# Rebuilding the FFN of a one-layer decoder step: fixed product banks, weight sums on VectorE, activations stored split

## The chip, the cores and the metric

The kernel runs on one core of a Trainium2 chip. The time is the device time of one execution in microseconds. The kernel before was timed in three runs: 3052.62, 3056.04 and 3064.1 us, the median 3056.04.

## The reference

One layer of a hybrid decoder is applied to 512 prompt tokens and to 32 sample tokens (8 sequences of 4) with the same weights; the model width is 2048 and everything is 32-bit floating point. Stick-breaking attention and a gated delta rule share one projection, cross-attention to a memory follows, then the feed-forward network (FFN), which alone changes here:

```python
hf = rmsnorm(x, p['norm_ffn_g'])
gate, up = jnp.split(hf @ p['w_gate_up'], 2, axis=-1)      # 2048 x 11264
x = x + (jax.nn.silu(gate) * up) @ p['w_down']             # 5632 x 2048
```

The kernel treats all 544 tokens (T) together, as two halves of 272 (HT), with features on the 128 partitions (P). There are 16 feature blocks of the model (KD) and 44 of the hidden layer (NH).

## The kernel before

Up to about 1505 us the kernel does the projections, the mixers and cross-attention; the change leaves these alone. The rest is the FFN.

**One wino.** The FFN multiplies 2x2 blocks by Winograd's form of Strassen's method: `wino` computes two blocks of columns of a weight matrix times all tokens, with seven products P1 to P7 instead of eight. Its inner dimension is given as a list of *pairs* of feature blocks. For each pair there are seven right operands (b11, b21, b22, and the sums t1 to t4), each of 128 x 272. For the weights `left` makes seven left operands: three are blocks of the matrix itself, four are sums s1 to s4. To get 32-bit accuracy from TensorE's fast format, each operand is kept as two exact parts, high and low, and each product is three matmuls: wh·bh, wh·bl, wl·bh.

**One unit.** `left` serves two pairs at a time: two DMAs of 256 KB on SP's queue into a tile `u`, four sums on POOL (L1613 to L1616), then two casts on ACT that give the high parts `wh` (L1620: 128x768 for the three blocks, 128x1024 for the four sums) and two subtractions on VectorE (DVE) that give the low parts `wl` (L1621, same shapes). The tiles of `wh` and `wl` have two buffers each. A unit is then 7 products x 2 pairs x 3 parts = 42 matmuls of 128x272 (L1647). There are 264 units.

**Gate-up.** 44 winos (j = 0 to 43), each over 8 pairs: 4 units, 168 matmuls. After each, `combine` (L1661 on ACT copies P1 out of PSUM; L1673 to L1679 on DVE add the other products) gives the gate and the up half, L1712 to L1715 apply scales and Silu. After each odd j two hidden blocks make a pair: POOL computes the sums t1 to t4 (`sums`, L1572 to L1575), and five transfers on ACT's queue store the pair in `hT` in DRAM, unsplit (L1719, L1721).

**Down.** The hidden pairs come in chunks of 4, 4, 4, 4 and 6 pairs (FFN_CHUNKS). For every chunk, 8 winos (m = 0, 2, ... 14) of two units (three in the last chunk) cover the 16 output blocks. `fetch` loads a pair from `hT` on SP's queue (L1696) and splits it again (L1590 on ACT, L1591 on DVE); two pairs of the next chunk are fetched at m = 4 and 10, the others at the chunk's end. From chunk 1 on `combine` adds the combined result to accumulators (DVE L1663 to L1669, POOL L1670 and L1671). In the last chunk the residual x is added on POOL, and `store_y` transposes, scales back and stores the blocks of the wino before.

**PSUM.** Eight banks: two buffers of a two-bank tile `mm`, and four one-bank buffers `aux`. The products lie in them as the code says:

```python
ma, mb = c.mm(), c.mm()
p4, p7, p3 = (c.aux()[:, :HT] for _ in range(3))
p1, p2, p6, p5 = ma[:, 0, :HT], ma[:, 1, :HT], mb[:, 0, :HT], mb[:, 1, :HT]
# (product, left operand, right operand)
todo = ((p1, 1, 0), (p2, 2, 1), (p4, 0, 6), (p6, 4, 4), (p5, 3, 3), (p7, 5, 5), (p3, 6, 2))
```

Each engine works through its own queue in order. A tile framework lays down that order and places the waits: an instruction waits for the last users of the tile's buffer that it writes, and for the writers of what it reads. `step` calls and priorities place the fetches and the next weights between the others.

Of the kernel before, what the change touches and what calls it, by code (L numbers as in the profile page):

```python
# [8 lines left out]
F32 = mybir.dt.float32  # L9
# [6 lines left out]
P = 128  # L16
# [17 lines left out]
PAIR_TAGS = [["ah"] * 7, ["ah"] * 5 + ["al"] * 2, ["al"] * 7, ["al"] * 3 + ["r"] * 4, ["ah"] * 4 + ["al"] * 3, ["al"] + ["h"] * 3 + ["t"] * 3, ["t"] * 7, ["t"] * 7]  # L34
# [36 lines left out]
def build_consts(c):  # L71
# [45 lines left out]
    # rows (head of two, 7 - batch, part, step) to columns (head of two, batch, step), both parts summed  # L117
# [4 lines left out]
    # rows (batch of four, part, head, step) to columns (head, batch of four, step): the head's own, both parts summed  # L122
# [17 lines left out]
def head_rows(c):  # L140
    """Per-head scalars: columns (chunk, head) on every partition, and two columns with rows (head, batch, step)."""
# [45 lines left out]
def weights(c, w, k0, nk, c0, n=P, kept=False, eng=None):  # L187
    """A block of weights, split exactly into two parts of 12 bits each: a pair for every feature block."""
# [13 lines left out]
def products(c, ps, w, k, act, first, last, n=P):  # L202
    """One block of a projection: w^T act, exact but for the product of the two low parts."""
# [11 lines left out]
def project(c, w, k0, c0, acts, n=P, step=8):  # L215
    """PSUM [n, 2, 272] = (rows k0.. of w, columns c0..c0+n)^T acts"""
# [14 lines left out]
def split(c, x, g, hi=None, lo=None):  # L231
    """x * g (g per partition) as two exact parts."""
# [13 lines left out]
class Stats:  # L246
    """Sum of squares over all features, for every token, on every partition."""
# [15 lines left out]
    def rstd(self, name, scale=None):  # L263
        """(mean + EPS) ** -0.5; with scale, what was added is scaled by it, and so is the root's reciprocal."""
# [81 lines left out]
def x_rstd(c, ss):  # L346
    """The reciprocal roots of the tokens' mean squares, from columns to rows on every partition."""
# [21 lines left out]
def first_projections(c):  # L369
    """Loads the tokens and projects them on the first head's q and k, feature block by feature block."""  # L370
# [20 lines left out]
class Side:  # L391
    """Work of the mixers, handed out in small steps between the blocks of the projections.

    A step yields (tensor engine time, time until its results are there), both estimates in us."""
# [6 lines left out]
    def put(self, g, low=False, tiles=None):  # L401
        """tiles: where the work takes its temporary tiles (float32, float32r) from, if not from the usual ones"""
# [51 lines left out]
    def finish(self, e, steps=1e9):  # L454
        """Runs one work to its end, or until so many of its steps are done."""
# [5 lines left out]
    def drain(self, some=None):  # L461
        """Runs all that is left, or until some is done."""
# [70 lines left out]
    # the sums of the keys behind, a block of keys after the other, each token's in its own column  # L533
# [21 lines left out]
def stick(c, z, n, sp=None):  # L555
    """softplus(z) and log(sigmoid(z)), each over n columns"""
# [18 lines left out]
def sb_sample(c, g):  # L575
    """Stick-breaking attention of the sample group, four heads: 512 paged keys and its own."""
# [12 lines left out]
    # own keys: rows (head, batch, step)  # L589
# [28 lines left out]
    # paged keys: columns (page, head, batch, step)  # L618
# [33 lines left out]
def parts(c, src, vector=True):  # L652
    """src [P, 512] as two exact parts."""
# [108 lines left out]
def load_pages(c, cache, pages, h0, nh):  # L762
    """[keys, (page, head, d)] of the given pages (indices into the table)."""
# [11 lines left out]
def gates(c, acts, rstd):  # L775
    """Decay and beta of the gated delta rule, with tokens on partitions."""
# [4 lines left out]
    # prompt: columns (a|b, chunk, head); sample: columns (a|b, stack), rows (head, batch, step)  # L781
# [28 lines left out]
    # running sums of log decay, totals, and their exponentials  # L810
# [22 lines left out]
    # per (head, batch) of the sample stacks, on every partition  # L833
# [7 lines left out]
def silu(c, x, out):  # L841
    """out = x * sigmoid(x), with exp and ln alone"""
# [1104 lines left out]
```

## Time and profile before

| | us |
|---|---|
| median of three runs | 3056.04 |
| span of the profiled execution (its own time beside which the parts are set) | 3059.9 |
| busy: PE / PE weight loads / DVE / ACT / POOL | 2900.2 / 2789.1 / 2134.3 / 1363.5 / 1671.8 |
| first to last start of the FFN's matmuls (L1647) | 1511.5 to 3047.9 |
| first to last copy of P1 in the gate-up (L1661, 44 of them) | 1545.4 to 2487.0 |

PE is TensorE, PEld its weight loads, which overlap the matmuls. A row of a group of instructions gives the line, the engine, the operation, the tiles (out<-in) and the shape, then the busy time and the mean duration in ns, then the idle time of the engine ahead of them and what ended it. A row of the timeline begins with the start in us from the span's start and the duration in us; what stands in brackets is the engine's idle time before, with the instruction that ended it. A row of a window gives its length, the busy time of PE, PEld, DVE, ACT and POOL with the number of instructions, the clock that TensorE was granted, the share of time in which the DMA engines were busy, and GB/s.

### The profile page before, as it was taken

What the parts mean: (1) busy time and instruction counts of PE and PEld (TensorE: products, weight loads), DVE (VectorE), ACT (ScalarE), POOL (GpSimd) and SP (SyncE); (2) the same over time, 40 slices, a digit from 0 to 9 for tenths busy, and PEclk for the clock granted to TensorE, in tenths of its full rate; (3) what the DMA queues carried; (4) which work ended last, traced back from release to release, by engine and by line L of the source; (5) the groups of instructions that cost most, each with busy time, mean ns of one, the idle gap of its engine ahead of it and who ended that gap; (6) DMA issues with size and microseconds to landing.
All of it is one profiled execution on the core that took longest, in us unless ns stands there. A gap on an engine that the chain in (4) does not pass through costs nothing.

```text
span 3059.9 us, 58347 instructions
## 1 busy us (share of the span) xinstructions
PE 2900.2 (95%) x22118; PEld 2789.1 (91%) x22118; DVE 2134.3 (70%) x3339; ACT 1363.5 (45%) x2600; POOL 1671.8 (55%) x1784
## 2 busy tenths in 40 slices
PE   8999999999999999999799999999999989988898
PEld 7999998889899999999689999999999989988797
DVE  6776775655655655366687777777777888888865
ACT  5544453435645654245543343333333344334333
POOL 3211122312112100032378988898888977999997
PEclk9999999999999999999899999999999999999999
DMA  7323233544535765423434344333434354344343
GB/s 212 95 80 85 75 88 99 144 137 147 173 105 151 227 197 150 127 81 116 161 117 127 118 122 123 121 117 118 125 118 123 116 179 132 110 131 127 119 137 105
DMA packets 619505, 392.67 MB, mean 128 GB/s; under 512 B 36475, under 2 KB 572360, under 8 KB 619224
## 3 DMA queue, kind: packets, MB, share of 16 engines
q1 hardware_dynamic: 596904, 355.95, 39.6%
q10 hardware_dynamic: 22320, 32.99, 3.0%
q8 instruction: 174, 2.85, 0.4%
q14 instruction: 107, 0.88, 0.1%
HBM read 334.17 MB, written 54.68 MB: 127 GB/s over the span
## 4 chain that ended last, share of the span: by engine, by line
POOL 27%; PE 20%; DVE 8%; issue 4%; DMA 4%; ACT 2%; SPq 0%; POOLq 0%; ACTq 0%; DVEq 0%
PE mm L208 7%; POOL u L1615 6%; POOL u L1613 6%; POOL u L1614 5%; PE mm L1647 5%; POOL u L1616 5%; PE aux L1647 4%; DVE wl L1621 3%; DMA u<-in_w_gate_up 2%; DVE pr L1591 2%; PE aux L1342 2%; POOL acc L1670 1%; PE mm L1530 1%; POOL x L1572 1%; PE aux L960 1%
## 5 line engine op out<-in xcount | busy, mean ns | idle before, releaser
L1621 DVE TENSOR_TENSOR wl<-u,wh 128x768 fp32r<-128x768 f32 (+1 forms) x528 | 752.5, 1442 | 315.9 <-ACT wh L1620 213.6
L1647 PE MATMUL mm<-pr,wh 128*128 128x272 f32 x4224 | 830.6, 292 | 41.6 <-DVE acc L1663 25.3
L1620 ACT CAST wh<-u 128x768 fp32r<-128x768 f32 (+1 forms) x528 | 488.8, 943 | 826.5 <-PE aux L1647 295.4
L1647 PEld LDWEIGHTS mm<-pr,wh 128*128 128x128 f32 x4224 | 669.4, 191 | 50.5 <-DVE acc L1663 20.3
L1647 PE MATMUL aux<-pr,wh 128*128 128x272 f32 x3168 | 626.9, 292 | 17.7 <-DVE acc L1669 6.7
L1647 PE MATMUL mm<-pr,wl 128*128 128x272 f32 x2112 | 615.7, 292 | 22.5 <-DVE wl L1621 22.5
L208 PE MATMUL mm<-ah,wh 128*128 128x272 f32 (+1 forms) x2464 | 538.6, 298 | 5.7 <-ACT ah L321 4.6
L1647 PEld LDWEIGHTS aux<-pr,wh 128*128 128x128 f32 x3168 | 506.8, 192 | 21.7 <-DVE acc L1669 8.6
L208 PE MATMUL mm<-al,wh 128*128 128x272 f32 (+1 forms) x2464 | 524.3, 291 | 0.7 <-DVE al L239 0.7
L208 PE MATMUL mm<-ah,wl 128*128 128x272 f32 (+1 forms) x2464 | 515.6, 290 | 0.1
L1647 PE MATMUL aux<-pr,wl 128*128 128x272 f32 x1584 | 460.9, 291 | 2.0 <-DVE wl L1621 2.0
L1647 PEld LDWEIGHTS mm<-pr,wl 128*128 128x128 f32 x2112 | 403.3, 191 | 28.4 <-DVE wl L1621 28.4
L208 PEld LDWEIGHTS mm<-ah,wh 128*128 128x128 f32 (+1 forms) x2464 | 391.9, 189 | 28.8 <-issue 8.5
L197 DVE TENSOR_TENSOR wl<-wr,wh 128x512 fp32r<-128x512 f32 (+1 forms) x366 | 264.0, 725 | 195.9 <-ACT wh L196 186.7
L208 PEld LDWEIGHTS mm<-al,wh 128*128 128x128 f32 (+1 forms) x2464 | 389.6, 188 | 5.4 <-issue 2.0
L208 PEld LDWEIGHTS mm<-ah,wl 128*128 128x128 f32 (+1 forms) x2464 | 386.2, 188 | 2.5 <-DVE wl L197 0.5
L196 ACT CAST wh<-wr 128x512 fp32r<-128x512 f32 (+1 forms) x366 | 224.3, 615 | 336.6 <-PE mm L208 272.6
L1613 POOL TENSOR_TENSOR u<-u 128x256 f32<-128x256 f32 x264 | 277.3, 1050 | 140.8 <-DMA u<-in_w_gate_up 90.2
L1615 POOL TENSOR_TENSOR u<-u 128x256 f32<-128x256 f32 x264 | 323.2, 1224 | 0.0
L1616 POOL TENSOR_TENSOR u<-u 128x256 f32<-128x256 f32 x264 | 308.5, 1169 | 19.1
L1647 PEld LDWEIGHTS aux<-pr,wl 128*128 128x128 f32 x1584 | 303.7, 192 | 2.6 <-DVE wl L1621 2.4
L1614 POOL TENSOR_TENSOR u<-u 128x256 f32<-128x256 f32 x264 | 270.4, 1024 | 0.0
(518 smaller groups left out, 3809.1 us busy)
## 6 DMA issues: line engine op xcount, KB each, us to landing
u<-in_w_gate_up SPq DMA_DIRECT2D x352, 256.0 KB
wr<-in_w_in SPq DMA_DIRECT2D x108, 512.0 KB
u<-in_w_down SPq DMA_DIRECT2D x176, 256.0 KB
v<-hT SPq DMA_DIRECT2D x66, 272.0 KB
page<-in_cache_sb_k SPq DMA_DIRECT2D x128, 128.0 KB
page<-in_cache_sb_v SPq DMA_DIRECT2D x64, 256.0 KB
wr<-in_w_out SPq DMA_DIRECT2D x32, 512.0 KB
hT<-x ACTq DMA_DIRECT2D x44, 272.0 KB
```

Source lines behind the costliest of these rows:

```text
L196: nc.scalar.copy(hi[:, :m, :n], raw[:, k : k + m, :n])
L197: nc.vector.tensor_sub(lo[:, :m, :n], raw[:, k : k + m, :n], hi[:, :m, :n].bitcast(F32))
L208: c.nc.tensor.matmul(ps[:n, h, :HT], l[:, :n], r[:, h * HT : (h + 1) * HT], start=first and i == 0, stop=last and i == 2,)
L1342: nc.tensor.matmul(ps[:, :256], l, r, start=k == 0 and n == 0, stop=k == 7 and n == 2)
L1591: nc.vector.tensor_sub(lo[:, o : o + n * HT], x[:, : n * HT], hi[:, : n * HT].bitcast(F32))
L1613: nc.gpsimd.tensor_add(s1, a21, a22)
L1614: nc.gpsimd.tensor_sub(s3, a11, a21)
L1615: nc.gpsimd.tensor_sub(s2, s1, a11)
L1616: nc.gpsimd.tensor_sub(s4, a12, s2)
L1620: nc.scalar.copy(hi, u[:, o : o + n])
L1621: nc.vector.tensor_sub(lo, u[:, o : o + n], hi.bitcast(F32))
L1647: nc.tensor.matmul(ps, l[:, cols], r, start=u + i == 0 and j == 0, stop=u + i == n - 1 and j == 2)
```

## The change

- **Fixed banks.** One PSUM tile `bank` of seven banks is allocated once and serves every wino; each product has its own bank. One bank is left for everything else (`aux`, one buffer). The order of the products becomes P1, P7, P6, P2, P5, P4, P3.
- **Combination.** In the gate-up one ACT copy (L1667) and five DVE additions (L1668 to L1672), two of them over two products at once.
- **Weight sums.** `left` has two tiles, `raw` and `sum`. Three of the four sums go to DVE (L1617, L1618, L1620), one stays on POOL (L1619).
- **Down projection.** The class `Sums` keeps all seven products of each wino apart in SBUF: four ACT copies in chunk 0 (L1689), four DVE additions straight from the banks in later chunks (L1693). The residual is added in chunk 1 (POOL), the combination is made once, in the last chunk (`finish`, DVE).
- **Stored parts.** POOL and ACT split a hidden pair before it is stored (`part_of` with POOL for the low parts), so `hT` holds seven tiles of 128x544 a pair, 42.9 MB in all instead of 21.4 MB written and read. `fetch` is seven DMAs of 272 KB straight into the operands' tiles, issued on POOL's queue (L1727), with no split behind them.

```diff
 def left(c, w, k, ca, cb):
-    u = c.wu.tile([P, 8, 2 * P], F32, tag="u", name="u", bufs=3)
+    a, b = (c.wu.tile([P, 4, 2 * P], F32, tag=x, name=x, bufs=n) for x, n in (("raw", 3), ("sum", 2)))
...
-    nc.gpsimd.tensor_add(s1, a21, a22)
-    nc.gpsimd.tensor_sub(s3, a11, a21)
-    nc.gpsimd.tensor_sub(s2, s1, a11)
-    nc.gpsimd.tensor_sub(s4, a12, s2)
+    nc.vector.tensor_sub(b[:, 2], a[:, 0], a[:, 2])
+    nc.vector.tensor_add(b[:, 1], b[:, 2], a[:, 1])
+    nc.gpsimd.tensor_add(b[:, 0], a[:, 0], a[:, 1])
+    nc.vector.tensor_sub(b[:, 3], a[:, 3], b[:, 1])
...
+P1, P6, P2, P3, P4, P5, P7 = range(7)
+PRODUCTS = ((P1, 1, 0), (P7, 5, 5), (P6, 4, 4), (P2, 2, 1), (P5, 3, 3), (P4, 0, 6), (P3, 6, 2))
...
-                    nc.tensor.matmul(ps, l[:, cols], r, start=u + i == 0 and j == 0, stop=u + i == n - 1 and j == 2)
+                    nc.tensor.matmul(
+                        c.bank[:, p, :HT], l[:, cols], r,
...
+def combine(c, y, z):
+    bank = c.bank[:, :, :HT]
+    b, e = c.tt("b"), c.tt("e")
+    s1, u2, u3, u4 = b[:, :HT], b[:, HT:], e[:, :HT], e[:, HT:]
+    nc.scalar.copy(s1, bank[:, P1])
+    nc.vector.tensor_add(u2, s1, bank[:, P6])
+    nc.vector.tensor_add(y[:, :HT], s1, bank[:, P2])
+    nc.vector.tensor_add(halves(e), bc(u2.rearrange("p (o x) -> p o x", o=1), [P, 2, HT]), bank[:, P7 : P5 - 1 : -1])
+    nc.vector.tensor_add(halves(z), bc(u3.rearrange("p (o x) -> p o x", o=1), [P, 2, HT]), bank[:, P4 : P5 + 1])
+    nc.vector.tensor_add(y[:, HT:], u4, bank[:, P3])
...
+class Sums:
...
+        self.parts = ((halves(self.a), P1, 2), (self.s.rearrange("p (o x) -> p o x", o=1), P7, 1), (halves(self.z), P4, 2), (halves(self.y), P2, 2))
+    def keep(self):
+        for x, b, n in self.parts:
+            self.c.nc.scalar.copy(x, self.c.bank[:, b : b + n, :HT])
+    def add(self):
+        for x, b, n in self.parts:
+            self.c.nc.vector.tensor_add(x, x, self.c.bank[:, b : b + n, :HT])
...
 def ffn(c, pairs, st, r1):
-    hT = c.dram.tile([NH // 2, P, 7 * HT], F32, name="hT")
+    hT = c.dram.tile([NH // 2, P, 7, T], F32, name="hT")
...
-                nc.sync.dma_start(v[:, : n * HT], src[:, o * HT : (o + n) * HT])
-                part_of(c, v, tags, n, ops)
+            for i, t in enumerate(tiles):
+                nc.gpsimd.dma_start(t, src[:, i])
...
-            for i, x in enumerate((v[1], *sums(c, *v, nc.gpsimd))):
-                nc.scalar.dma_start(dst[:, (2 * i + 1) * HT : (2 * i + 3) * HT], x)
+            for i, x in enumerate((*v, *sums(c, *v, nc.gpsimd))):
+                hi, lo, n, _ = part_of(c, x, lambda: c.hp.tile([P, T], F32R, tag="st", name="hs", bufs=4), 2 if i else 1, nc.gpsimd)
+                for t in (hi, lo)[2 - n :]:
+                    nc.scalar.dma_start(hT[j // 2, :, len(tiles)], t[:, :].bitcast(F32))
...
+            if ci == 0:
+                acc.append(Sums(c, m // 2))
+                acc[-1].keep()
+            else:
+                acc[m // 2].add()
...
+    c.bank = banks.tile([P, 7, 512], F32, name="bank")
+    c.aux = lambda: banks.tile([P, 512], F32, tag="aux", name="aux", bufs=1)
```

How the order of instructions moves is seen at the boundary between two winos of the gate-up. In a row, `pr` is a right operand, the tile ahead of the arrow is written, and brackets name the counters that are waited for (DVE_49 counts DVE's instructions, and so on). On TensorE before, the last matmuls of one wino and the first of the next, up to the next wait, stand so:

```order
L1647 MATMUL aux<-pr,wh 128x272 x2
L1647 MATMUL aux<-pr,wl 128x272
L1647 MATMUL mm<-pr,wh 128x272 [waits DVE_49,Activation_49]
L1647 MATMUL mm<-pr,wh 128x272
L1647 MATMUL mm<-pr,wl 128x272
...
L1647 MATMUL mm<-pr,wh 128x272 [waits DVE_49]
```

The first wait for DVE is met by L1674, the reader of the old P2, the second, 18 matmuls later, by L1677. After the change the same place reads:

```order
L1652 MATMUL bank<-pr,wh 128x272 x2
L1652 MATMUL bank<-pr,wl 128x272
L1652 MATMUL bank<-pr,wh 128x272 [waits DVE_49,Activation_49]
L1652 MATMUL bank<-pr,wh 128x272
L1652 MATMUL bank<-pr,wl 128x272
```

The single wait has moved to the first matmul for all seven products, and its count is that of L1672, the last operation of the combination before. On DVE before, around the combination of a gate-up wino:

```order
L1621 TENSOR_TENSOR wl<-u,wh 128x1024 [waits PE_49,Activation_49]
L1621 TENSOR_TENSOR wl<-u,wh 128x768 [waits DMAHW0_49,DMAHW1_49,PE_49,Activation_49]
L1673 TENSOR_TENSOR b<-g,mm 128x272 [waits PE_49]
L1674 TENSOR_TENSOR g<-g,mm 128x272 [waits DVE_49]
L1675 TENSOR_TENSOR g<-b,mm 128x272
L1676 TENSOR_TENSOR b<-b,aux 128x272 [waits PE_49]
L1679 TENSOR_TENSOR g<-g,aux 128x272 [waits DVE_49,PE_49]
```

Only the next wino's 128x768 subtraction stands between. On DVE after, `raw` and `sum` being the weight tiles and `e` and `b` scratch tiles:

```order
L1620 TENSOR_TENSOR sum<-raw,sum 128x256 [waits DVE_49]
L1625 TENSOR_TENSOR wl<-raw,wh 128x768 [waits PE_49,Activation_49]
L1625 TENSOR_TENSOR wl<-sum,wh 128x1024 [waits PE_49,Activation_49]
L1668 TENSOR_TENSOR b<-b,bank 128x272 [waits Activation_49]
L1669 TENSOR_TENSOR g<-b,bank 128x272
L1670 TENSOR_TENSOR e<-b,bank 128x544 [waits DVE_49]
L1617 TENSOR_TENSOR sum<-raw 128x256 [waits DMAHW3_49,DMAHW2_49]
L1671 TENSOR_TENSOR u<-e,bank 128x544 [waits DVE_49]
L1672 TENSOR_TENSOR g<-e,bank 128x272
```

Both subtractions of the next wino's second unit now stand ahead of the combination, and a weight sum within it. On ACT after, at the same place:

```order
L1624 CAST wh<-raw 128x768 [waits DMAHW6_49,DMAHW7_49,DVE_49,PE_49]
L1624 CAST wh<-sum 128x1024 [waits DVE_49,PE_49,Pool_49]
L1667 COPY b<-bank 128x272 [waits PE_49]
L1743 ACTIVATE g<-g 128x544 [waits DVE_49]
```

The copy of P1 stands behind both casts and waits for the last matmul of the wino, which writes P3. In the down projection the 128x768 subtraction stands ahead of the four additions L1693 and the 128x1024 one behind them.

More of the change, by code (lines that the diff above doesn't have):

```diff
@@ L1704, in ffn @@
         step = (lambda u: fetch(0, 2, nxt)) if j == NH - 1 else None
-        p = wino(c, c.w_gu, 0, k * P, HID + k * P, pairs, step, 0 if j else EARLY)
+        wino(c, c.w_gu, 0, k * P, HID + k * P, pairs, step, 0 if j else EARLY)
         if j == 0:
@@ L1730, in step @@
             def step(u):
-                if m == KD - 2 and u < 2:
-                    fetch(ci + 1, 1 if len(DOWN_PLAN[ci]) == 4 else 2, nxt)
+                if m == KD - 2 and u == 0:
+                    fetch(ci + 1, 2, nxt)
                 if m in (4, 10) and u == 0:
@@ L1738, in step @@
                         store_y(c, done, u)
-            p = wino(c, c.w_down, 2 * first[ci], m * P, (m + 1) * P, pairs, step)
+            wino(c, c.w_down, 2 * first[ci], m * P, (m + 1) * P, pairs, step)
             if ci == 0:
-                acc += [c.tt("acc") for _ in range(2)]
-            if last:
-                x = c.wu.tile([P, 2, T], F32, tag="u", name="xl", bufs=3)
-                nc.sync.dma_start(x, c.xT[m : m + 2].rearrange("k p t -> p k t"))
-                for i in range(2):
-                    nc.gpsimd.tensor_add(acc[m + i], acc[m + i], x[:, i])
-            combine(c, p, *acc[m : m + 2], None if ci == 0 else nc.vector if last and m == KD - 2 else nc.gpsimd)
-            if last:
-                done = [(m + i, acc[m + i]) for i in range(2)]
+                acc.append(Sums(c, m // 2))
+                acc[-1].keep()
+            else:
+                acc[m // 2].add()
+            if ci == 1:
+                x = [c.cst.tile([P, T], F32, tag="rstd", name="xl", bufs=2) for _ in range(2)]
+                for i in range(2):
+                    nc.sync.dma_start(x[i], c.xT[m + i])
+                acc[m // 2].residual(*x)
+            if last:
+                acc[m // 2].finish()
+                done = [(m, acc[m // 2].y), (m + 1, acc[m // 2].z)]
     for u in range(3):
```

117 lines of the change are left out of this document (54 added, 63 removed).

## The prediction

> **What bounds the kernel now.** I read the page first: the engines' busy shares, then the slices of the span.
>
> ```profile
> span 3059.9 us, 58347 instructions
> PE 2900.2 (95%) x22118; PEld 2789.1 (91%) x22118; DVE 2134.3 (70%) x3339; ACT 1363.5 (45%) x2600; POOL 1671.8 (55%) x1784
> PE   8999999999999999999799999999999989988898
> POOL 3211122312112100032378988898888977999997
> ```
>
> TensorE is busy 95% of the span, POOL nearly all of the second half. Every edit lies in the last half, the FFN; so next come the matmul line's rows (min/median/max ns, first to last start) and the windows.
>
> ```profile
> L1647 PE MATMUL aux<-pr,wh x3168: 282/288/597, 1511.5 to 3047.8; 128*128 128x272 f32 x198
> 3047.89 0.29 PE L1647 MATMUL aux<-pr,wl 128*128 128x272 f32 x1
> L1661 ACT COPY g<-mm x44: 377/386/388, 1545.4 to 2487.0; 128x272 f32<-128x272 f32 x44
> core 0: us, PE busy (x) PEld busy (x) DVE busy (x) ACT busy (x) POOL busy (x), PEclk, DMA share, GB/s
> 1700.30:1714.93 14.63, 14.63 (x119) 14.63 (x118) 11.28 (x14) 3.71 (x6) 14.39 (x14) 1.00 0.30 93
> 1900.00:2100.00 200.00, 196.56 (x1560) 195.27 (x1559) 155.50 (x170) 76.98 (x93) 181.68 (x168) 1.00 0.38 116
> 2700.00:2900.00 200.00, 178.02 (x1334) 174.35 (x1333) 173.08 (x204) 78.81 (x111) 193.44 (x158) 0.95 0.42 123
> ```
>
> An uninterrupted stretch issues 119 matmuls in 14.63 us, one or two of them hanging over its edges: 0.125 us each. The FFN has 264 units of 42, 11,088 matmuls: 1386 us at that pace. It takes 1511.5 to 3048.2, 1536.7 us, so 151 us are lost. Hardly any of that is in the gate-up: 44 copies from 1545.4 to 2487.0 are 21.9 us a wino, against 168 x 0.125 = 21.0. A tuned pace leaves at most 0.9 us a wino to gain; the down projection (178 of 200 us) has more.
>
> What keeps TensorE fed at a gate-up boundary is shown by one of them:
>
> ```profile
> 1722.94 0.39 ACT L1661 COPY g<-mm 128x272 f32<-128x272 f32 x1 [0.54 <-PE mm L1647]
> 1725.52 0.42 DVE L1673 TENSOR_TENSOR b<-g,mm 128x272 f32<-128x272 f32 x1
> 1725.98 0.44 DVE L1674 TENSOR_TENSOR g<-g,mm 128x272 f32<-128x272 f32 x1
> 1726.38 0.28 PE L1647 MATMUL aux<-pr,wl 128*128 128x272 f32 x1
> 1726.57 0.49 PE L1647 MATMUL mm<-pr,wh 128*128 128x272 f32 x2
> 1727.73 0.43 DVE L1678 TENSOR_TENSOR u<-b,aux 128x272 f32<-128x272 f32 x1
> ```
>
> The copy of P1 and the reading of P2 (L1674) are over when the wino's last matmul starts (1726.38); the next wino starts 0.19 us later, into the other buffer, while VectorE combines until 1728.16.
>
> **The change at a boundary: the term that decides.** After it all seven products live in one tile, `bank`. By the order, the first matmul of each wino carries the only wait on it: in the gate-up for L1672, the last operation of the combination before; in the down projection for the last L1693 (chunk 0: L1689). The copy L1667 in turn waits for the wino's last matmul. Thus matmuls and combination alternate. Worse, two instructions that themselves need the last unit's buffers back stand ahead: ACT has the next wino's 128x1024 cast ahead of L1667, and VectorE its 128x1024 subtraction ahead of L1668, in 42 of 44 winos.
>
> ```profile
> L1620 ACT CAST wh<-u 128x1024 fp32r<-128x1024 f32 x138 | 144.9, 1050 | 376.7 <-POOL x L1575 119.2 <-PE aux L1647 110.9 <-DVE u L1715 53.3
> L1621 DVE TENSOR_TENSOR wl<-u,wh 128x1024 fp32r<-128x1024 f32 x138 | 214.0, 1551 | 146.7 <-POOL u L1614 76.9 <-ACT wh L1620 68.7
> L1621 DVE TENSOR_TENSOR wl<-u,wh 128x768 fp32r<-128x768 f32 x138 | 173.9, 1260 | 25.0 <-ACT wh L1620 25.0
> 1529.54 0.94 DVE L1621 TENSOR_TENSOR wl<-u,wh 128x768 fp32r<-128x768 f32 x1
> 2486.62 1.21 DVE L1621 TENSOR_TENSOR wl<-u,wh 128x1024 fp32r<-128x1024 f32 x1
> 3050.11 0.44 DVE L1663 TENSOR_TENSOR acc<-acc,mm 128x272 f32<-128x272 f32 x1 [0.76 <-ACT a L1661]
> 3050.46 0.43 DVE L1665 TENSOR_TENSOR b<-a,mm 128x272 f32<-128x272 f32 x1
> ...
> 3051.85 0.72 DVE L1670 TENSOR_TENSOR acc<-acc,a 128x544 f32<-128x544 f32 x1
> 3052.49 0.72 DVE L1671 TENSOR_TENSOR acc<-acc,b 128x544 f32<-128x544 f32 x1
> ```
>
> Queued one behind another, VectorE starts a 272 every 0.35 us and a 544 every 0.64 (the tail's starts), some 0.08 under their durations; an unhindered 1024 is then 1.13 and a 768 0.86. From the last matmul's end: cast 1.05 with its hop 1.1; subtraction to 2.25; L1668 and L1669 0.35 each, L1670 0.64, L1617 of the next weights 0.33 (a 256, by the 272), L1671 0.64, L1672 0.43: 5.0, and TensorE resumes near 5.05. Counted from the last start instead of the end, 5.2 us are lost.
>
> What does such a gap do to the clock? Before has four:
>
> ```profile
> 2491.89 0.57 PE L1647 MATMUL mm<-pr,wh 128*128 128x272 f32 x1 [6.54 <-DVE g L1674]
> 2610.88 0.52 PE L1647 MATMUL mm<-pr,wh 128*128 128x272 f32 x2 [2.46 <-DVE acc L1663]
> 2906.81 0.60 PE L1647 MATMUL aux<-pr,wh 128*128 128x272 f32 x1 [2.99 <-DVE pr L1591]
> 2506.91 0.52 PE L1647 MATMUL mm<-pr,wh 128*128 128x272 f32 x2 [1.60 <-DVE acc L1674]
> 2492.00:2496.00 4.00, 4.00 (x18) 4.00 (x19) 4.00 (x8) 1.53 (x3) 3.87 (x5) 0.51 0.61 180
> 2612.00:2615.00 3.00, 3.00 (x16) 3.00 (x15) 3.00 (x7) 0.72 (x1) 2.12 (x2) 0.50 0.53 156
> 2906.80:2910.80 4.00, 3.99 (x17) 3.99 (x18) 4.00 (x5) 0.83 (x1) 1.54 (x3) 0.50 0.52 139
> 2507.00:2511.00 4.00, 4.00 (x32) 4.00 (x33) 4.00 (x7) 1.38 (x2) 3.92 (x5) 1.00 0.28 107
> ```
>
> After gaps of 6.54, 2.46 and 2.99 us the granted clock is 0.50 to 0.51 for some 3 to 4 us; after 1.60 it stays 1.00. The price: 18 matmuls in 4 us where 32 fit (14 x 0.125 = 1.75 us), 16 of 24 (1.0), 17 of 32 (1.9). I take 1.75 behind the 5-us gaps, 1.4 (the mean of the other two) behind shorter ones. The 6.54-us gap is moreover this very mechanism: TensorE waited for L1674, the reader of a product's bank. The Trainium skill ("TensorE: Matmul & The Clock Gate", Part 1, on oscillation) speaks against the change likewise: a wait for each tile that crosses the monitor's window, about 3.4 us, makes each tile start at half rate. The trace agrees for 6.54 us, but shows half rate already after 2.46.
>
> **The sum, part by part.**
> - Gate-up: 5.2 + 1.75, and 0.3 for odd winos, where ACT's casts of the stored operands wait for POOL's sums (ACT waited 119.2 us for POOL's L1575 above): 7.25, say 7.2 x 44 = 317 us lost. Bounds: subtraction at its contended mean 1.55 and each 544 and 256 stretched by the same 1.28: about +1.2; without the clock's share -1.75.
> - Down, chunks 0 to 3: here the 1024 subtraction stands behind the adds, the 768 one ahead. It ends near 0.95 after the last matmul (its cast needs the last but one product); adds 0.64, 0.35, 0.64, 0.72: 3.3; lost 3.5 + 1.4 = 4.9, x 32 = 157. ACT's copies in chunk 0 (one 272 took 0.386 us, L1661) come to the same.
> - Last chunk: four adds stay and L1706 on follow off the path, but TensorE's transposes share the one `aux` bank that is left, and their evictions stand among casts and adds: a gap of 4.1, clock 1.6, 0.5 of stalls inside: 6.2 x 8 = 50.
> - Stored parts: a pair is seven 272-KB tiles, not four loads of one or two halves; the down projection's splits (ACT, VectorE) go, the transfers double:
>
> ```profile
> v<-hT SPq DMA_DIRECT2D x66, 272.0 KB
> hT<-x ACTq DMA_DIRECT2D x44, 272.0 KB
> 2486.00:2492.00 6.00, 0.11 (x1) 0.14 (x1) 6.00 (x10) 4.26 (x8) 3.59 (x3) 0.76 0.97 296
> 1505.00:1560.00 55.00, 40.70 (x277) 38.38 (x277) 52.83 (x77) 38.02 (x64) 32.09 (x31) 0.91 0.29 94
> L1613 POOL TENSOR_TENSOR u<-u 128x256 f32<-128x256 f32 x138 | 153.6, 1113 | 62.8 <-DMA u<-in_w_gate_up 62.3 <-DVE u L1678 0.4
> ```
>
>   Four pairs are 28 x 0.279 = 7.8 MB; at the 296 GB/s of the fullest stretch, less a third for weights, 40 us. Chunks 1 to 3 fetch two pairs early, at m = 4 and 10; two come at the end, some 20 us within two 10.5-us winos, and POOL's issues, each waiting for the one eight before, hold back the weight sum L1619 queued behind. I take 10 for the first transition, 6.5 for each of three, 20 into the six-pair chunk: 50; ends 0 (hidden) and 100 (every fetch exposed). POOL's issues of DMAs have no row: between nothing and one POOL operation (1.11), 154 x 1.11 = 171 us of a queue that keeps spare time, so inside those ends. The Trainium skill ("Advanced Engine Details and Errata", DGE: Hardware vs Software) gives about 1 us to the first byte for POOL's way and 600 ns for the others: estimated 0.4 us a load, 2 us over five transitions; no run here shows it.
> - Weight sums: POOL loses three of its four adds a unit. VectorE a gate-up wino: 4 x (0.86 + 1.13), 12 x 0.33, combination 2.3, three 544s of gating 1.9 = 16.2 us unhindered; 21 if all of it is stretched by 1.3, as the two means above are (1.55 of 1.21, 1.26 of 0.94). Beside a 28-us wino that is hidden; beside 21.0 it would be the bound. Nothing is gained: POOL, busy 181.68 of 200 us, stopped TensorE (196.56) hardly at all. Before's stalls, up to 0.9 a wino, go, since the casts are now done in the wait.
> - Start: P1's first copy, 1545.4, is 132 matmuls (16.5 us) + 17.4 behind 1511.5; VectorE, busy 52.83 of 55 us there, gets more sums and POOL (32.09) fewer; I leave it at 17, 5 either way. Tail +1 (six more adds after the last product, against two 544s saved).
>
> Losses 17 + 317 + 157 + 50 + 50 = 591, against 151: +440, tail +1. On the span 3059.9: 3501. The runs' median, 3056.04, is 0.13% under that span, so I say 3500. About 0.5% can be told from no change here.
>
> **Rivals.**
> 1. The clock does not drop each time. By that same window (free-running, one whole idle one needed; as the page has it) 3.3-us gaps would cost none and 5.05-us ones every second time. Worked out from rows: 22 x 1.75 + 32 x 1.4 + 8 x 1.6 = 96 less, 3405. Against it: half clock after 2.46 and 2.99 us. 15%.
> 2. Transitions and the store chain are heavier: the bounds +1.2 x 44 = 53 and +50 for fetches give 3550 to 3605. For it: 296 GB/s at a DMA share of 0.97 before, with half the data. 18%.
> 3. The other side: banks come free one by one, P1's once it is copied. Then the gate-up's 44 x 0.9 = 40 us and half of what is left for the down projection (151 - 17 - 40 = 94) are recovered: about 2970. It decides if a product's matmuls wait only for that product's reader; and VectorE stays under 21.0 a wino (16.2 to 21). Against it: one wait a wino, for the last reader. 4%.
> 4. The change does nothing to the time, wait and gains cancelling within 15 us: 2%.
>
> **How the numbers follow.** Forecast 61%, rivals 15, 18, 4 and 2. Range 3390 to 3600: it takes in the first rival and most of the second, and leaves about two in ten out. Faster 0.04, same 0.02, slower 0.94.
>
> **What would show it.** Gate-up winos 28 us apart by the copies of P1, not 21.9; before each wino's first matmul an idle 5 us put down to VectorE L1672 (3.3 us, L1693, in the down projection); a granted clock near 0.87 over the gate-up, TensorE busy under 85%; POOL clearly under 55%. Gaps under 2 us at the boundaries, or the first matmul waiting for the copy alone, would prove me wrong; so would full clock behind the gaps (3405).

## The result, and the profile after

| | us |
|---|---|
| before, median of the runs on this chip | 3057.98 |
| after, median of four runs (3491.34 to 3499.72) | 3493.83 |
| forecast, with its range | 3500 (3390 to 3600) |

The ratio after to before is 1.1422, 95% interval 1.1401 to 1.1442: the change costs 436 us. The page after, the lines that answer to those of before:

```profile
span 3491.8 us, 58372 instructions
PE 3043.1 (87%) x22118; PEld 2925.7 (84%) x22118; DVE 2234.6 (64%) x3849; ACT 1367.0 (39%) x2592; POOL 859.2 (25%) x1180
PE   8999999999999999978888888888888877877887
POOL 3211222121210002233232322222323334512221
PEclk9999999999999999989888888888888889888898
```

TensorE drops to 87% of the span, with the same number of matmuls, and to eight tenths in nearly every slice of the FFN; its granted clock drops there too. POOL falls from 55 to 25%, and that buys nothing. Who TensorE waits for is told by the list of its waits from 1500 us on (waited for, us in total, times, longest):

```profile
PE bank L1652 <- DVE g L1672: 219.4, 43, 5.3
PE bank L1652 <- DVE a L1693: 81.3, 28, 3.4
PE bank L1652 <- ACT a L1689: 24.9, 8, 4.7
PE bank L1652 <- DMA pr<-hT: 0.4, 1, 0.4
L1667 ACT COPY b<-bank x44: 378/379/386, 1548.8 to 2793.9; 128x272 f32<-128x272 f32 x44
```

43 boundaries between gate-up winos, each with one wait for the last reader of the bank; 28 in the down projection for the last addition; 8 for the last copy. For a load of stored parts it waits 0.4 us in all. The last row gives the pace: 43 steps from 1548.8 to 2793.9 are 28.96 us a wino (21.9 before). One boundary in the timeline:

```profile
1807.48 1.04 ACT L1624 CAST wh<-sum 128x1024 fp32r<-128x1024 f32 x1
1808.43 0.38 ACT L1667 COPY b<-bank 128x272 f32<-128x272 f32 x1
1808.55 1.23 DVE L1625 TENSOR_TENSOR wl<-sum,wh 128x1024 fp32r<-128x1024 f32 x1
1809.70 0.43 DVE L1668 TENSOR_TENSOR b<-b,bank 128x272 f32<-128x272 f32 x1
1810.05 0.43 DVE L1669 TENSOR_TENSOR g<-b,bank 128x272 f32<-128x272 f32 x1
1810.39 0.71 DVE L1670 TENSOR_TENSOR e<-b,bank 128x544 f32<-128x544 f32 x1
1811.02 0.56 DVE L1617 TENSOR_TENSOR sum<-raw 128x256 f32<-128x256 f32 x1
1811.51 0.71 DVE L1671 TENSOR_TENSOR u<-e,bank 128x544 f32<-128x544 f32 x1
1812.14 0.43 DVE L1672 TENSOR_TENSOR g<-e,bank 128x272 f32<-128x272 f32 x1
1812.71 0.79 PE L1652 MATMUL bank<-pr,wh 128*128 128x272 f32 x2 [5.19 <-DVE g L1672]
```

Read downwards it is the forecast's chain: the next weights' cast, then the copy of P1 behind it on ACT; the next weights' subtraction, then the combination behind it on VectorE, with a weight sum in the middle; then TensorE.

### The profile page after: what moved, and what is told of

Same layout as the page of the kernel before. It is cut to its first block, busy times and chain, and to the rows that moved or that the text cites. A ratio compares the mean times of both kernels' runs of the same rounds, so it can differ in the third digit from the quotient of the medians.

```text
span 3491.8 us, 58372 instructions
## 1 busy us (share of the span) xinstructions
PE 3043.1 (87%) x22118; PEld 2925.7 (84%) x22118; DVE 2234.6 (64%) x3849; ACT 1367.0 (39%) x2592; POOL 859.2 (25%) x1180
## 4 chain that ended last, share of the span: by engine, by line
PE 47%; DVE 10%; ACT 4%; POOL 3%; issue 2%; DMA 2%; ACTq 0%; SPq 0%; POOLq 0%; DVEq 0%
PE bank L1652 36%; PE mm L208 6%; ACT wh L1624 3%; DVE wl L1625 3%; POOL hs L1595 2%; DVE a L1693 2%; PE aux L1342 1%; PE mm L1530 1%; DVE e L1670 1%; DVE u L1671 1%; PE aux L960 1%; DMA pr<-hT 1%; DVE sum L1617 1%; ACT hs L1594 0%; DVE g L1672 0%
## 5 line engine op out<-in xcount | busy, mean ns | idle before, releaser
L1652 PE MATMUL bank<-pr,wh 128*128 128x272 f32 x7392 | 1554.1, 310 | 344.5 <-DVE g L1672 219.4
L1652 PEld LDWEIGHTS bank<-pr,wh 128*128 128x128 f32 x7392 | 1289.8, 209 | 363.4 <-issue 317.1
L1652 PE MATMUL bank<-pr,wl 128*128 128x272 f32 x3696 | 1136.5, 307 | 21.4 <-DVE wl L1625 21.3
L1652 PEld LDWEIGHTS bank<-pr,wl 128*128 128x128 f32 x3696 | 770.4, 208 | 27.1 <-DVE wl L1625 27.1
L1625 DVE TENSOR_TENSOR wl<-raw,wh 128x768 fp32r<-128x768 f32 x264 | 266.9, 1011 | 586.0 <-PE bank L1652 388.6
L1624 ACT CAST wh<-raw 128x768 fp32r<-128x768 f32 x264 | 220.1, 834 | 929.0 <-PE bank L1652 906.2
L1619 POOL TENSOR_TENSOR sum<-raw 128x256 f32<-128x256 f32 x264 | 264.0, 1000 | 1071.4 <-DVE wl L1625 1041.6
L208 PEld LDWEIGHTS mm<-ah,wh 128*128 128x128 f32 (+1 forms) x2464 | 390.8, 188 | 27.5 <-issue 8.5
L1625 DVE TENSOR_TENSOR wl<-sum,wh 128x1024 fp32r<-128x1024 f32 x264 | 340.8, 1291 | 25.1 <-ACT wh L1624 17.6
L1624 ACT CAST wh<-sum 128x1024 fp32r<-128x1024 f32 x264 | 276.8, 1049 | 43.0 <-PE bank L1652 24.2
L1618 DVE TENSOR_TENSOR sum<-sum,raw 128x256 f32<-128x256 f32 x264 | 180.6, 691 | 5.7
L1617 DVE TENSOR_TENSOR sum<-raw 128x256 f32<-128x256 f32 x264 | 133.1, 510 | 27.5 <-DMA raw<-in_w_down 20.6
L1620 DVE TENSOR_TENSOR sum<-raw,sum 128x256 f32<-128x256 f32 x264 | 117.3, 451 | 7.3
L1743 ACT ACTIVATE g<-g 128x544 f32<-128x544 f32 x44 | 28.9, 657 | 214.8 <-DVE g L1742 214.8
L1727 POOL DMA_DIRECT2D pr<-hT x154 | 82.7, 558 | 49.1 <-PE bank L1652 29.0
```

The lines of the kernel that those rows point to most:

```text
L208: c.nc.tensor.matmul(ps[:n, h, :HT], l[:, :n], r[:, h * HT : (h + 1) * HT], start=first and i == 0, stop=last and i == 2,)
L1617: nc.vector.tensor_sub(b[:, 2], a[:, 0], a[:, 2])
L1618: nc.vector.tensor_add(b[:, 1], b[:, 2], a[:, 1])
L1619: nc.gpsimd.tensor_add(b[:, 0], a[:, 0], a[:, 1])
L1620: nc.vector.tensor_sub(b[:, 3], a[:, 3], b[:, 1])
L1624: nc.scalar.copy(hi, x)
```

## Experiments

Each kernel was run beside the kernel before on the same chip, whose median there was between 3058 and 3061 us; the ratio is to those runs. Line numbers are those of each run's own kernel. e2 and e3 were timed in two runs each, the others in four or more. "A wino" is the mean step between the copies of P1 in the gate-up.

| kernel | median us | ratio to before (95%) | a wino |
|---|---|---|---|
| before | 3057.98 | | 21.90 |
| the change | 3493.83 | 1.142 (1.140 to 1.144) | 28.96 |
| e1_apart | 3079.75 | 1.006 (1.004 to 1.009) | 23.10 |
| e2_fill | 3418.73 | 1.117 (1.114 to 1.120) | 27.10 |
| e3_last | 3412.32 | 1.115 (1.112 to 1.118) | 28.58 |
| e4_sums | 3073.0 | 1.005 (1.003 to 1.006) | 22.33 |
| e5_stored | 3106.05 | 1.016 (1.014 to 1.017) | 22.19 |
| e6_pool | 3199.1 | 1.046 (1.044 to 1.048) | 25.11 |
| e9_half | 3082.0 | 1.008 (1.006 to 1.009) | 23.20 |
| e10_three | 3131.85 | 1.024 (1.023 to 1.026) | 23.91 |
| e11_chain | 3085.1 | 1.008 (1.006 to 1.010) | 23.35 |
| e12_chain_half | 3110.36 | 1.017 (1.015 to 1.019) | 23.93 |
| e13_mixed | 3057.36 | 1.000 (0.999 to 1.001) | 22.37 |
| e14_tsums | 3059.97 | 1.001 (1.000 to 1.001) | 22.41 |

### Is it the one tile? (e1_apart)

```diff
-    c.bank = banks.tile([P, 7, 512], F32, name="bank")
+    c.bank = [banks.tile([P, 512], F32, name=f"bank{i}") for i in range(7)]
...
-    nc.vector.tensor_add(halves(e), bc(u2...), bank[:, P7 : P5 - 1 : -1])
+    nc.vector.tensor_add(u3, u2, bank[P7])
+    nc.vector.tensor_add(u4, u2, bank[P5])
```

> The changed kernel, but the seven banks are seven tiles of one bank each instead of one tile, so each product's matmuls wait only for that product's reader (the additions over two banks become two of 272). Theory (the wait on the whole tile is the cost, with the clock drop behind it): no idle 5 us at the boundaries, gate-up winos 21.0 to 21.9 us apart instead of 28.96, granted clock back near 1, about 2990 us (2950 to 3060). Rival (VectorE with three weight sums a unit, 19 us busy in each 28.96-us wino, or the doubled transfers are the bound): still above 3200.

Measured: 3079.75 us, so 414 of the 436 us go with the tile's partition alone; every other part of the change is still there (the combination's additions and copies over two banks become two over one each). The rival, above 3200 us, is refuted. The 43 waits for the combination's last addition are gone. Of the waits for the copies and additions of the down projection (L1692 and L1696 here) 10.1 us are left, of 106:

```profile
PE bank L1652 <- ACT a L1692: 8.9, 2, 6.3
PE bank L1652 <- DVE a L1696: 1.2, 2, 0.8
```

But the time is 20 us above the forecast range of this run, and 0.6% above before. Gate-up and down projection part company: a wino takes 23.10 us (23.10 - 21.90, times 43, is 52 us lost), while from the last copy of P1 to the last matmul it is 527.9 us (2537.8 to 3065.7) against 560.9 before: 33 gained. What holds the gate-up, from 1600 to 2400 us (first the window with the busy times, then TensorE's waits), and what ACT does after an odd wino:

```profile
1600.00:2400.00 800.00, 758.74 (x5835) 747.58 (x5835) 721.89 (x1040) 324.57 (x416) 300.55 (x276) 0.98 0.43 134
PE bank L1652 <- DVE wl L1625: 34.3, 34, 1.1
1808.25 4.75 ACTq L1755 DMA_DIRECT2D hT<-hs  x2
1813.04 0.65 ACT L1594 CAST hs<-x 128x544 fp32r<-128x544 f32 x1 [4.82 <-POOL hs L1595]
1813.59 0.83 ACT L1624 CAST wh<-raw 128x768 fp32r<-128x768 f32 x1
1818.79 0.39 PE L1652 MATMUL bank<-pr,wl 128*128 128x272 f32 x1 [1.09 <-DVE wl L1625]
```

Two things are to be seen: VectorE is busy 722 of 800 us, and ACT's queue stands still for 4.75 us at the store of a hidden pair, waiting for POOL's low part, with the next weight cast behind it; the weights then come late. In the change itself the wait at the boundary covered most of this: within a wino TensorE's waits for weights were 0.6 to 1.0 us, in every second one. The next runs take these two apart.

### How much of the 7 us a wino is the clock (e2_fill)

```diff
+    if fill:
+        ps = c.aux()
+        x = pairs[0][0][0]
+        for i in range(fill):
+            nc.tensor.matmul(ps[:, :HT], x[:, :P], x, start=i == 0, stop=i == fill - 1)
```

> The changed kernel with 40 matmuls of 128x272 on operands at hand into the spare bank, read by nobody, behind the last matmul of every gate-up wino but the last: TensorE is busy during its wait. Theory (28.96 us a wino are 21.0 of matmuls, 5.2 of wait and some 2.1 of half clock): the clock stays 1.00, winos 26.6 to 27.0 apart, 43 x 2.0 to 2.4 less, 3390 to 3410 us. Rival (the 2 us are refilling and waits for weights, not the clock): 3480 to 3500, and the first matmuls of a wino still come 0.23 us apart.

Measured: 27.10 us a wino, 1.86 less than the change, and 3418.73 us, 75 less. The granted clock over the gate-up (the column ahead of the DMA share) is whole again:

```profile
1600.00:2400.00 800.00, 788.38 (x6197) 778.69 (x6197) 580.18 (x836) 275.92 (x354) 221.03 (x235) 1.00 0.36 114
1581.64:2770.05 1188.41, 964.72 (x6889) 952.22 (x6889) 788.52 (x1149) 383.83 (x493) 318.13 (x330) 0.88 0.34 108
```

The first row is this kernel, the second the change. The clock is thus worth 1.86 us of the 7 a wino, a little under the 2.0 to 2.4 expected, and the time lands 9 us above that range. Part of the shortfall lies in the edit: at the last two boundaries the wait is hardly filled, since 11 of the useless matmuls stand in the one and none in the other (L1677 here is the change's L1672):

```profile
2666.86 0.49 PE L1652 MATMUL bank<-pr,wh 128*128 128x272 f32 x2 [3.82 <-DVE g L1677]
2695.84 0.56 PE L1652 MATMUL bank<-pr,wh 128*128 128x272 f32 x1 [5.05 <-DVE g L1677]
```

Where it is filled, the steps from wino to wino are 26.5 and 27.5 us in turns, against 28.9 and 29.1 in the change: the clock is worth 2.0 us there. Work of no use in the wait is faster than waiting.

### What stands ahead in the queues (e3_last)

```diff
-                for j, (l, r) in enumerate(((wh, bh), (wh, bl), (wl, bh))):
+                for j, (l, r) in enumerate(((wh, bh), (wl, bh), (wh, bl))):
```

> The changed kernel with the three parts of each product in the order wh bh, wl bh, wh bl, nothing else in the source: the 128x1024 cast now becomes ready no earlier than the copy of P1 and stands behind it; on VectorE L1668 to L1670 stand ahead of the 128x1024 subtraction, in the down projection all four additions ahead of both subtractions. Theory (what stands ahead in the queues sets the length of the wait): in the gate-up the wait falls from 5.1 to about 4.1 us (the subtraction still comes ahead of L1671), in the down projection from 3.4 to 2.4: 44 x 1.0 + 24 x 1.0 less, about 3425 us (3400 to 3450). Rival (the wait is the combination alone): no change, 3485 to 3500.

Measured: 3412.32 us, 82 less than the change for exchanging two of the three parts, inside the range, but not as divided: the gate-up's wait fell only to 4.8 us (L1668 there still follows the 128x768 subtraction), worth 0.38 us a wino or 16 us; the rest came from the down projection, where the wait fell from 3.4 to 2.5 us and from 2.9 to 2.0 in chunk 0, and often took the clock's drop along: half clock stood behind 6 of the 20 waits of 2.47 to 2.52 us. The last chunk gave 10 us of the 82. The clock behind the 2.02-us waits of chunk 0:

```profile
2829.39:2831.39 2.00, 2.00 (x16) 2.00 (x17) 1.08 (x1) 0.89 (x1) 0.00 (x0) 1.00 0.86 254
2842.21:2844.21 2.00, 2.00 (x9) 2.00 (x10) 1.08 (x1) 0.89 (x1) 0.00 (x0) 0.52 0.84 251
2856.56:2858.56 2.00, 2.00 (x16) 2.00 (x17) 1.08 (x1) 0.89 (x1) 0.00 (x0) 1.00 0.85 251
2869.38:2871.38 2.00, 2.00 (x9) 2.00 (x10) 1.08 (x1) 0.89 (x1) 0.00 (x0) 0.56 0.81 242
```

Equal waits, and the clock stays whole or falls to half in strict turns, in all seven of them: the length alone does not decide.

### The parts by themselves (e4_sums, e5_stored)

e4 puts the changed `left` (two tiles, three sums on VectorE) into the kernel before:

```diff
-    nc.gpsimd.tensor_sub(s3, a11, a21)
-    nc.gpsimd.tensor_sub(s2, s1, a11)
-    nc.gpsimd.tensor_sub(s4, a12, s2)
+    nc.vector.tensor_sub(b[:, 2], a[:, 0], a[:, 2])
+    nc.vector.tensor_add(b[:, 1], b[:, 2], a[:, 1])
+    nc.vector.tensor_sub(b[:, 3], a[:, 3], b[:, 1])
```

e5 puts the stored parts there:

```diff
-                nc.sync.dma_start(v[:, : n * HT], src[:, o * HT : (o + n) * HT])
-                part_of(c, v, tags, n, ops)
+            for i, t in enumerate(tiles):
+                nc.gpsimd.dma_start(t, src[:, i])
```

In both, t3 keeps before's sign, which does not belong to the new sums, so what they compute is not the layer; the amount of work is the same.

> The kernel before with only the weight sums of the change (two tiles, three sums on VectorE, one on POOL). By the prediction nothing is gained, POOL did not stop TensorE; VectorE's 155.5 us in 200 become about 17.0 + 12 x 0.55 less 2 of contention = 21.6 us a wino, just over the 21.0 of TensorE: 3050 to 3090 us. Rival one (POOL was the hidden limit): 3000 to 3030. Rival two (VectorE is plainly the bound, each weight late): above 3120.

> The kernel before with only the stored parts of the change: high and low parts stored and fetched straight into the operands on POOL's queue (low parts subtracted on VectorE ahead of the store), weight tiles as in the change to make room, all sums on POOL, product buffers and combination as before. Theory (the fetch's splits stood ahead of the combination at each chunk's end, which is where before waits 4.6 to 7.4 us; the doubled transfers are hidden for the most part): those waits shrink, down projection some 25 us shorter, gate-up within 10 us: 3035 us (3020 to 3055). Rival (the doubled transfers cost more at the chunks' ends than the splits): above 3080.

Measured: e4 3073.0 us, inside its range: POOL goes from 719 to 240 us busy in the 800 from 1600 to 2400 us, and the kernel is 0.5% slower, since the combination on VectorE now comes late (first row below, TensorE's wait for it in the same 800 us; before, 0.9 us). e5 3106.05, 51 us above its range and on the rival's side. Its down projection waits for the loads themselves (the other rows, TensorE's waits from 2490 us on):

```profile
PE mm L1647 <- DVE g L1674: 33.2, 35, 1.3
PE aux L1651 <- DMA pr<-hT: 14.1, 10, 3.9
PE mm L1651 <- DMA pr<-hT: 12.5, 3, 4.5
PE mm L1651 <- DVE acc L1667: 22.7, 13, 8.4
```

Before, TensorE waits for no load directly there. In e5 POOL also has all weight sums and the additions to the accumulators, and the loads are issued from its queue between these; that this makes them late is likely, but was not tried by itself. The waits for the combination (8.4 us the longest) stay as well. In e1, where POOL is freer, loads cost 14.6 us in all. So neither of these two parts alone brings a gain. The 33 us that e1 gains in the down projection appear with the seven banks, the additions per product and the freer POOL together; which share each has, and whether all are needed, was not tried.

### VectorE's load or ACT's queue (e6, e9, e10, e11, e12)

All start from e1. e6, e9 and e10 move weight sums back to POOL (all; s4; three of four, with one on VectorE):

```diff
-    nc.vector.tensor_sub(b[:, 3], a[:, 3], b[:, 1])
+    nc.gpsimd.tensor_sub(b[:, 3], a[:, 3], b[:, 1])
```

> Seven one-bank tiles as in e1, and all four weight sums back on POOL. In e1 VectorE is busy 181 of 200 us of the gate-up, a wino 23.1 us. Theory (the three sums make VectorE the bound there; POOL with all sums and the low parts of the store needs 19.7 + 2.7 = 22.4 us a wino and is the next bound): winos 22.0 to 22.6 us apart, 44 x 0.7 = 30 less than e1, 3050 us (3030 to 3065). Rival (not VectorE but the seven tiles' waits or the transfers hold the gate-up at 23.1): 3075 to 3085.

> Seven one-bank tiles as in e1, weight sums two on VectorE and two on POOL (the last, s4, moved). Theory: VectorE loses 4 x 0.7 us a wino of 20.9 busy, POOL stays under 17, so TensorE bounds again: winos 21.3 to 21.7 apart, 44 x 1.6 = 70 less than e1, 3010 us (2990 to 3030), faster than before. Rival (VectorE's queue order, not its load, holds it): above 3050.

> Seven one-bank tiles as in e1, weight sums three on POOL and one on VectorE. Theory: POOL 12 x 1.05 + 4.3 = 17 us a wino, VectorE some 15: TensorE bounds, winos 21.3 to 21.6 apart, 3005 us (2990 to 3025). Rival (POOL's three dependent sums come late for the 128x1024 cast): 21.9 or more apart, above 3030.

All three missed: e9 and e10 came out on their rivals' side, e6 above its theory and its rival both. e9 takes VectorE from 722 to 670 us busy in the 800 and changes nothing (23.20 us a wino): the load alone was not what stopped e1. e10 and e6 are slower, 23.91 and 25.11 us, because ACT's weight casts now wait longer for POOL, and TensorE for them; in e6 16 times, some 4 us each. The rows are TensorE's wait in e6, then what ACT waited for in e6 and in e1, from 1600 to 2400 us:

```profile
PE bank L1652 <- ACT wh L1624: 64.0, 16, 4.3
ACT wh L1624 <- POOL hs L1595: 100.5, 25, 4.8
ACT wh L1624 <- POOL hs L1595: 33.5, 26, 2.1
```

e11 takes the store's chain off ACT, and e12 adds e9's move:

```diff
-    c.nc.scalar.copy(hi[:, : n * HT], x[:, : n * HT])
+    (eng.tensor_copy if eng is c.nc.gpsimd else c.nc.scalar.copy)(hi[:, : n * HT], x[:, : n * HT])
...
-                    nc.scalar.dma_start(hT[j // 2, :, len(tiles)], t[:, :].bitcast(F32))
+                    nc.gpsimd.dma_start(hT[j // 2, :, len(tiles)], t[:, :].bitcast(F32))
```

> Seven one-bank tiles as in e1, and the store of a hidden pair wholly on POOL: it makes the high parts (L1594, ACT before) and issues the seven stores (ACT's queue before). In e1 a weight cast on ACT stands behind the store's casts and issues, which wait for POOL 5 us and more after every odd wino, and the weights then come late (stalls of 0.9, 0.4 and 1.1 us within 3 us). Theory (this queueing, not VectorE's load, keeps e1's gate-up at 23.1 us a wino): 21.2 to 21.9 a wino, 44 x 1.5 = 66 less, 3012 us (2990 to 3035), faster than before. Rival (VectorE, 181 of 200 us busy, is the bound after all): 3060 to 3085.

> As e11_chain, with the sum s4 on POOL as in e9. Theory: with the queueing gone VectorE's load shows: 4 x 0.7 us less of it a wino, 0 to 20 us under e11_chain (2990 to 3015). Rival (POOL, now with store chain and eight sums a wino, is late for the 128x1024 cast): 10 to 60 us over e11_chain.

Measured: 23.35 and 23.93 us a wino, no gain either; e12 is 25 us over e11, as its rival said. The first half of e11's theory held: VectorE's subtractions hardly wait for ACT's casts any more. But VectorE is now the bound, busy 788 of 800 us. The rows are the 128x768 subtraction of e1, then that and the window of e11, then the same two of e9:

```profile
L1625 DVE TENSOR_TENSOR wl<-raw,wh 128x768 fp32r<-128x768 f32 x140 | 142.4, 1017 | 44.3 <-ACT wh L1624 26.1 <-PE bank L1652 18.2
L1625 DVE TENSOR_TENSOR wl<-raw,wh 128x768 fp32r<-128x768 f32 x137 | 180.1, 1315 | 1.7 <-ACT wh L1624 1.5
1600.00:2400.00 800.00, 751.47 (x5778) 743.33 (x5777) 787.54 (x1033) 290.60 (x345) 416.90 (x462) 0.97 0.43 132
L1625 DVE TENSOR_TENSOR wl<-raw,wh 128x768 fp32r<-128x768 f32 x139 | 157.7, 1134 | 97.2 <-ACT wh L1624 67.5 <-PE bank L1652 29.7
1600.00:2400.00 800.00, 757.82 (x5828) 746.67 (x5828) 670.28 (x900) 325.98 (x416) 414.17 (x415) 0.98 0.43 134
```

The same subtraction takes 1017 ns in e1, where POOL is busy 301 us, and 1315 in e11, where it is busy 417. In e9 POOL is just as busy, 414 us, and the subtraction takes 1134: what POOL does counts, and not only for how long. So work handed to POOL comes back as longer operations on VectorE. It seems that e1's gate-up has two limits that lie close together, ACT's queue behind the store and VectorE with the three sums. This is inferred: e12 eases both, but there ACT's casts wait 98.5 us of the 800 for POOL's sum s4.

### A better division (e13_mixed, e14_tsums)

e13 divides by stage: sums on POOL in the gate-up, on VectorE in the down projection, low parts of the store on VectorE. e14 also moves the pair's sums t1 to t4 to VectorE.

```diff
+    eng = c.nc.gpsimd if w is c.w_gu else c.nc.vector
...
-    nc.vector.tensor_sub(b[:, 2], a[:, 0], a[:, 2])
+    eng.tensor_sub(b[:, 2], a[:, 0], a[:, 2])
...
-            for i, x in enumerate((*v, *sums(c, *v, nc.gpsimd))):
+            for i, x in enumerate((*v, *sums(c, *v, nc.vector))):
```

> Seven one-bank tiles as in e1; in the gate-up all weight sums on POOL and the low parts of the store on VectorE, in the down projection the change's division (three sums on VectorE). Theory (VectorE and POOL slow each other, so each needs slack where it stands on the path: e11 showed VectorE 98% busy with three sums and a busier POOL, e6 POOL too slow with sums and low parts; e5's division gave 22.2 us a wino in the gate-up, e1's down projection took some 530 us): gate-up 21.6 to 22.2 a wino, 3030 us (3010 to 3050), the first that is faster than before. Rival (in ACT's queue the weight casts still stand behind the store's casts, which wait for POOL's sums): 22.8 or more a wino, above 3070.

> As e13_mixed, with the hidden pair's sums t1 to t4 (L1572 to L1575) on VectorE instead of POOL, so that ACT's casts for the store no longer wait for POOL behind its weight sums (3.3 us in e13, with weight casts queued behind). Theory: the odd winos' stalls of about 2 us go, gate-up 21.5 to 21.9 a wino instead of 22.4, 44 x 0.6 = 26 less than e13: 3030 us (3015 to 3045), faster than before. Rival (VectorE, 163 of 200 us busy in e13, passes the wait on): 3050 to 3065.

Measured: 3057.36 and 3059.97 us, both the same as the before beside them within 0.15%, and both above their ranges. In e13 a gate-up wino is 22.37 us, above its forecast and between the two theories; the down projection keeps most of e1's gain (2509.1 to 3043.0, 533.9 us). In e14 the casts wait no longer for POOL but for VectorE's low parts, and the time is the same, as its rival said. No version tried is measurably faster than the kernel before.

## Why the prediction was right, point by point

The parts of the sum, with what the profile after gives for each (its first FFN matmul starts at 1508.8, the first wino ends at 1547.7, the last gate-up matmul ends at 2793.7, chunk 1 begins at 2920.4, the last chunk at 3305.4, the last matmul ends at 3478.2; 0.125 us a matmul taken off):

| lost, us | forecast | measured |
|---|---|---|
| start | 17 | 18 |
| gate-up, 43 boundaries | 317 | 343 |
| chunk 0 with the first transition | 39 + 10 | 43 |
| chunks 1 to 3 with their transitions | 118 + 20 | 133 |
| last chunk with its transition | 50 + 20 | 47 |
| all | 591 | 584 |

That the total is met within 7 us is partly luck: the gate-up lost 26 us more than forecast, and the rows below it together 34 us less.

- The gate-up wait was forecast as 5.05 us: it is about 5.04 and 5.19 in turns. The step held in its place, its length and its order. The cause is shown by e1: one tile for seven products.
- Of the signs to look for, the winos came 28.96 us apart and the clock was 0.88 over the gate-up; TensorE was busy 81% there (964.72 of 1188.41 us), but 87% of the whole span.
- The down projection's wait, 3.3 us by forecast, is 3.37, and 2.88 in chunk 0. There I took ACT's copies to come to the same; they are 0.5 us shorter, having no subtraction ahead of them.
- The clock term was mis-sized both ways. In the gate-up it was 1.75 us by forecast; by e2 it is 1.86, and 2.0 where the wait was filled. In chunks 1 to 3 it was 1.4 by forecast, but half clock stood behind every one of the 24 waits of 3.3 to 3.7 us; a wino took 16.06 us (2920.41 to 3289.79 over 23), so the term is some 2 us there. In chunk 0 the first two of the seven waits of 2.88 us still left half clock behind them, the last five cost no clock at all, and a wino then took 13.65 us. The windows, chunk 0 from its fifth wino on, then chunks 1 to 3:

```profile
2865.82:2920.41 54.59, 43.06 (x337) 42.18 (x337) 30.47 (x39) 22.06 (x32) 14.41 (x22) 1.00 0.44 125
2950.28:3289.79 339.51, 268.32 (x1765) 264.33 (x1765) 223.34 (x295) 77.40 (x84) 99.06 (x119) 0.85 0.42 122
```

- The price of a gap came from four gaps of before. Its FFN has more: of the ten from 2.1 us up, nine left half clock behind them, but one of 2.74 us did not (its row, then the 3.4 us from there). A row of before thus already showed that a shorter wait need not cost clock, as the last five of chunk 0 did not.

```profile
1537.82 0.73 PE L270 MATMUL aux<-acc,ones 128*128 128x272 f32 x2 [2.74 <-POOL acc L260]
1537.82:1541.22 3.40, 1.77 (x11) 1.48 (x11) 3.40 (x6) 2.89 (x5) 0.00 (x0) 1.00 0.00 0
```

- The last chunk's gap, one of 4.1 us by forecast, comes as two, of 1.66 and 1.19 us, with TensorE's transposes between them. Half clock stood behind four of six such pairs. One of them:

```profile
3457.48 0.39 PE L1816 MATMUL aux<-ident,a 128*32 128x128 f32 x2 [1.66 <-ACT y L1811]
3459.07 0.59 PE L1652 MATMUL bank<-pr,wh 128*128 128x272 f32 x1 [1.19 <-DVE a L1693]
```

- The first rival (3405) is refuted as I wrote it, since 3.37-us waits always cost clock, and those of about 5.1 us every time and not every second one. The row where it is nearer than the forecast is chunk 0. The Trainium skill ("TensorE: Matmul & The Clock Gate", Part 1) speaks of an activity window of about 3.4 us that runs freely, and of half rate after at least one such window of idling. The trace fits the free running, since waits of one length, 2.88 us, went both ways. It does not agree that a whole window of idling is needed: the 24 waits of 3.3 to 3.7 us all dropped the clock, and those of 2.02 us did so every second time (e3).
- The transitions were too dear: 50 us by forecast. Beside the waits at the boundaries, TensorE waited 0.4 us in all for a load, and at the first transition some 4 us more for late weights and a late copy. The loads had POOL's queue nearly to themselves (859 us busy in all, and 0.56 us for each of the 154 issues); that the longer winos covered them is likely, but was not tried by itself.
- The second rival (3550 to 3605) put its weight on those transitions and the store chain; the chain exists (e1), but in the change it lies inside the wait.
- The third rival, 2970 us if the banks come free one by one, was right about the wait, as e1 shows, but wrong by 110 us in its time: e1 gives 3080. I let it recover the gate-up's stalls as well; instead VectorE's work and the store's queue, which the sum counts as hidden beside a 28-us wino, come out into the open as soon as a wino could take 21 us. The prediction had said of VectorE's sums that beside 21.0 they would be the bound; the store's queue it had priced at 0.3 us a wino.
- POOL's relief was worth nothing, as forecast: 0.5% slower in e4, where it stands alone.

## What to carry to other kernels

Ask of every buffer what the smallest thing is that a wait can tell apart: joining tiles that are released at different times into one makes the first writer wait for the last reader, and nothing in the arithmetic shows it, while the order's waits do. When a wait at a boundary is found, look also at what stands ahead of the releasing instruction in its queue: here 2 of 5 us were the next wino's weights, and the exchange of two of a product's three matmuls moved 82 us. And a part that is hidden beside a slowed stage has to be priced again for the stage at full pace.

## What the runs showed of the hardware

TensorE's clock fell to half behind all 42 waits of about 5.1 us in the change's gate-up and all 24 of 3.3 to 3.7 us in its chunks 1 to 3. Behind waits of 2.0 to 3.1 us it fell sometimes: in strict turns behind 2.02 us (e3), behind the first two waits of 2.88 us and then not behind five that came 13.65 us apart (the change), behind one of 3.06 us and not behind one of 3.05 (e3). So the length alone does not decide; that it is the moment at which a wait begins is inferred. Useless matmuls in the wait kept the clock whole and gained 75 us (e2).

VectorE's subtraction of two SBUF operands grew by 29% (1017 to 1315 ns) when POOL took over the store's casts and issues (e11), and by 12% (to 1134) when POOL, as long busy, took over a weight sum (e9). In the change, each DMA issued on POOL's queue took 0.53 to 0.76 us of POOL's time:

```profile
L1727 POOL DMA_DIRECT2D pr<-hT x154: 527/557/763, 2771.4 to 3316.6; - x154
```
